# Dilated attention: near scores in the far scores' 64x32 tiles, scores and turns as one chain a block, values once per four blocks, bias as two loads a head

## The chip, the core and the metric

The kernel runs on one core of one Trainium2 chip. A core has a matrix engine (TensorE, "PE" in the profile; its weight loads are "PEld"), three engines for elementwise work (VectorE "DVE", ScalarE "ACT", GpSimd "POOL"), a queue that issues nearly all DMAs here (SyncE, "SP"), and 16 DMA engines that carry them. The metric is the device time of one execution in microseconds (us). Runs of one kernel are not equal: the three runs of the kernel before lie between 1393.0 and 1410.5 us.

## The reference

One block of a network on 1024 tokens of width 1024: a modulation from a condition vector, a norm, a projection into attention heads and gated delta-net heads, an output projection, and a gated feed-forward part. The change lies in the attention: 8 heads of 64, each with three dilated windows over the same keys, joined by a softmax over their log-sums. Cut to that:

```python
DILATED_BRANCHES = ((128, 1), (512, 4), (2048, 16))
...
def _dilated_branch(q, k, v, rel_bias, window, dilation):
    ...
    s = jnp.einsum('bhrnqd,bhrnkd->bhrnqk', qb * dh ** -0.5, kw) + bias[None, :, None, None]
    s = jnp.where(valid, s, NEG_INF)
    m = jnp.max(s, axis=-1, keepdims=True)
    e = jnp.exp(s - m)
    denom = jnp.sum(e, axis=-1, keepdims=True)
    o = jnp.einsum('bhrnqk,bhrnkd->bhrnqd', e, vw) / denom
    lse = (m + jnp.log(denom))[..., 0]
...
    w = jax.nn.softmax(jnp.stack(lses), axis=0)
    o = jnp.sum(w[..., None] * jnp.stack(outs), axis=0)
```

The three branches together are one softmax in which a key that lies in several windows counts several times. The kernel computes it so: score plus a bias that holds the relative bias and the logarithm of the count, one exponential, one sum, one product with the values.

## The kernel before

Everything is float32. Large products run as three matmuls of a split into high and low parts ("gemm", L575). The attention is worked in 4 pairs of heads, and in each pair in 8 blocks of 128 queries: 32 blocks. Heads 0 and 1 of a pair (`e` in the code) lie in partitions 0 to 63 and 64 to 127 of the tiles `q` and `k`. Within a block the 128 tokens are stored by class: token 4j + r stands at position 32r + j.

A block goes through three functions.

- `att_score` (L1317) makes the scores. A block's *near* keys are its own 128 and the 128 before: one matmul a head (L1330), a 64x128 tile of the array and 256 columns (128 in block 0). From block 2 on there are *far* keys, which only reach queries of their own class: four matmuls a head (L1336), each a 64x32 tile of one class r and 32n columns for block n. In the profile each such float32 matmul is two instructions. Then DVE adds the bias tile `bt` and takes a minimum (L1344, the scores are negated), ACT makes the exponential and the sum (L1348), DVE the reciprocal (L1349), POOL scales (L1350). The result is a tile `X` a head. Scores take their PSUM banks in turn from three.
- `att_turn` (L1358) transposes the pieces of `X` on PE (L1367, one to four a head and block) and copies them out of PSUM into a tile `et` (L1368; ACT for head 0 of the pair, DVE for head 1).
- `att_value` (L1373) multiplies with the values (L1399): parts of the near keys with `va`, parts of the far keys, class by class, with `vf`. It is called after every second block; the near parts of two blocks each time, the far parts of four blocks every second time. Four blocks share one PSUM bank, and after each four the bank is copied out (L1412 or L1416 and L1417).

`attend` (L1419) runs over 35 steps: the score of block i, the turn of block i - 1 (AT = 1), the values of block i - 3 (AV = 3). Before each step the function `ahead` puts a portion of gemm work into the program: projections that are left over, later the output projection (`out_delta`). A scheduler orders the instructions of each engine at compile time by the program's order and by what is ready. `tc.issue_after(x)` puts an instruction behind `x` on its engine; `urgent()` lets one go ahead of others. In `att_score` the matmuls of a block hang on each other in this way, in the order far classes, near head 0, near head 1; the matmuls of a value call as well; the turns do not.

The bias comes from a table. A matmul makes a row of 1152 values a head (L179), DVE negates it, three stores put it into HBM (`R_d`, L329). Eight copies within HBM write each head's row 32 times (`Rb_d`, L1124; from 70.7 us on in the profile). `att_bias` (L1273) then loads a head's tile `bt` from there with 15 DMAs (L1280), one of them for the far part (L1282), whose source address pattern leads with four repeats of the same rows. `att_load` (L1290) fetches q, k, the bias, `va` and `vf` for a pair; the next pair's load is called from the third block of a pair on. The values were stored by `va_evac` (L1088, stores at L1095), two stores a block of tokens and half.

Long before, between 68 and 111 us, the weights `wr_qd` and `wr_kd` of the delta-net's projections are loaded (L214), cast by ACT (L215) and completed by POOL (L216); between these casts ACT and POOL make the parts `hh` and `hl` of the normed input (L454, L461, L464).

Of the kernel before, what the change touches and what calls it, by code (L numbers as in the profile page):

```python
# [36 lines left out]
XB, ETB, AT, AV = 6, 4, 1, 3  # L37
# [31 lines left out]
def build(tc, I, out):  # L69
# [91 lines left out]
    tbl = start("tbl", "qd", [33, T]), start("tbl2", "qd", [33, P])  # L161
# [4 lines left out]
    for t, cs in zip(tbl, (slice(0, T), slice(T, T + P))):  # L166
        nc.sync.dma_start(t, I["tbl"][:, cs])
# [5 lines left out]
    R_d = dr.tile([8, 1152], F32, name="R_d")  # L173
    Rb_d = dr.tile([8, 32, 1152], F32, name="Rb_d")
    Rss = []
    for j in range(3):
        n = min(HALF, 1152 - HALF * j)
        ps = tbank(f"ps_R{j}")
        nc.tensor.matmul(  # L179
            ps[:8, 0:n], rb, tbl[j // 2][:, HALF * (j % 2) : HALF * (j % 2) + n], start=True, stop=True  # L180
        )
# [144 lines left out]
    for j, Rs in enumerate(Rss):  # L326
        n = min(HALF, 1152 - HALF * j)
        with tc.issue_after(loads[0].ins):
            nc.sync.dma_start(R_d[:, HALF * j : HALF * j + n], Rs[:, 0:n])  # L329
# [185 lines left out]
    class _:  # L515
        qk = scratch("qk", 8, [P, T])
        va = scratch("va", 2, [2, P, TB, P])
# [570 lines left out]
    def va_evac(c):  # L1088
        def f(tb, ps):
            t = pv.tile([P, 256], F32, name=f"va{c}_{tb}", tag="ev", bufs=4)  # L1090
            with urgent():
                taken[0] = nc.scalar.copy(t, ps[:, 0:256])
            with held():
                for i in range(2):
                    nc.sync.dma_start(  # L1095
                        bass.AP(
                            tensor=_.va[c].tensor, offset=_.va[c][i, 0:1, tb].offset,
                            ap=[[TB * P, 32], [32 * TB * P, 4], [1, P]],
                        ),
                        t[:, i * P : i * P + P],  # L1100
                    )
        return f
# [15 lines left out]
    def va_end(c):  # L1118
        f = va_evac(c)

        def g(tb, ps):
            f(tb, ps)
            if c == 0:
                nc.sync.dma_start(Rb_d[tb], R_d[tb : tb + 1, :].to_broadcast([32, 1152]))  # L1124
# [148 lines left out]
    def att_bias(h):  # L1273

        bt = pa.tile([P, HALF], F32, name=f"bt{h}", tag="bt", bufs=4)
        nc.gpsimd.memset(bt[:, 192:224], BIG)
        base, W = _.R[h, 0:1, :].offset, 1152

        def load(dst, at, ap):
            nc.sync.dma_start(dst, bass.AP(tensor=_.R.tensor, offset=base + at, ap=ap))  # L1280

        load(bt[:, 0:192], 3 * 288 + 31, [[0, 4], [W - 1, 32], [1, 192]])  # L1282
        for r in range(4):
            near = bt[32 * r : 32 * r + 32, 224:480].rearrange("p (d r j) -> p r d j", d=2, r=4)
            for a, b, at in ((0, r + 1, (3 - r) * 288 + 223), (r + 1, 4, 224)):
                for d in range(2 if a < b else 0):
                    load(near[:, a:b, d], at + 32 * d, [[W - 1, 32], [288, b - a], [1, 32]])
        return bt

    def att_load(hp):  # L1290
# [4 lines left out]
        bts = [att_bias(2 * hp + e) for e in range(2)]  # L1295
        va = pa.tile([P, TB, P], F32, name=f"va{hp}", tag="va", bufs=2)
        src = _.va[hp // 2][hp % 2]
        nc.sync.dma_start(va, src)
        vf = pa.tile([P, 2, 4, P], F32, name=f"vf{hp}", tag="vf", bufs=2)
        for c in range(2):  # L1300
            for n in range(4 - 2 * c):
                nc.sync.dma_start(
                    vf[32 * n : 32 * n + 32, c],
                    bass.AP(
                        tensor=src.tensor, offset=src[0:1, 4 * c + n].offset,
                        ap=[[TB * P, 32], [32 * TB * P, 4], [1, P]],
                    ),
                )
        return q, k, va, vf, bts
# [7 lines left out]
    def att_score(hp, n):  # L1317

        q, k, va, vf, bts = loaded[hp]
# [3 lines left out]
        rows = [slice(64 * e, 64 * e + 64) for e in range(2)]  # L1323
        parts = [(r, e) for r in (range(4) if f else ()) for e in range(2)] + [(None, 0), (None, 1)]
        mm = None
        with turn(f"S{hp}_{n}"):
            for r, e in parts:
                with tc.issue_after(mm.ins) if mm else ExitStack():
                    if r is None:
                        mm = nc.tensor.matmul(  # L1330
                            pss[e][:, f:w], q[rows[e], n * P : n * P + P], k[rows[e], b0 * P : n * P + P],
                            start=True, stop=True,
                        )
                    else:
                        qs = slice(32 * r, 32 * r + 32)
                        mm = nc.tensor.matmul(  # L1336
                            pss[e][qs, 0:f].rearrange("p (m j) -> p m j", j=32),
                            by_class(q[rows[e]])[:, n, r], by_class(k[rows[e]])[:, 0:n, r], start=True, stop=True,
                        )
        X = []  # L1340
        for e in range(2):
# [3 lines left out]
                out=x[:, 0:w], in0=pss[e][:, 0:w], in1=bts[e][:, 480 - w : 480], scale=1.0, scalar=3e38,  # L1345
# [8 lines left out]
        return X  # L1354
# [3 lines left out]
    def att_turn(hp, n, e, X):  # L1358
        h, f = 2 * hp + e, far(n)
        if n % 4 == 0:  # L1360
            turned[h] = pa.tile([P, 4, 4, P], F32, name=f"et{h}_{n // 4}", tag="et", bufs=ETB)
        s0, s1 = (1, 2) if n == 0 else (0, 2 + (n > 1) + (n > 5))
        cols = {0: f, 1: f + (P if n else 0), 2: 0, 3: P}
        ps = tbank(f"tr{h}_{n}")
        with turn(f"et{h}_{n}"):
            for i in range(s0, s1):
                nc.tensor.transpose(ps[:, i * P : i * P + P], X[:, cols[i] : cols[i] + P], ident)  # L1367
        (nc.vector.tensor_copy if e else nc.scalar.copy)(  # L1368
            turned[h][:, n % 4, s0:s1].rearrange("p b q -> p (b q)"), ps[:, s0 * P : s1 * P]
        )  # L1370
        return turned[h]

    def att_value(hp, n, ets):  # L1373

        q, k, va, vf, bts = loaded[hp]
        if n % 4 == 1:
            ybanks[hp] = ybank(f"y{hp}_{n}")
        yps = ybanks[hp]
# [3 lines left out]
        for m in (n - 1, n):  # L1382
            for i in range(0 if m else 1, 2):
                parts.append((slice(0, P), lambda e, b=m - 1 + i: va[:, b, 64 * e : 64 * e + 64],
                              m % 4, lambda e, m=m, i=i: ets[e][:, m % 4, i]))
        if n % 4 == 3:
            for c, n0, kr in ((0, 2 - 2 * half, 64 + 64 * half), (1, 2, 64))[: 1 + half]:
                for r in range(4):
                    qs = slice(32 * r, 32 * r + 32)
                    parts.append((slice(0, kr), lambda e, c=c, r=r: vf[:, c, r, 64 * e : 64 * e + 64],  # L1390
                                  (slice(n0, 4), qs), lambda e, n0=n0, c=c, qs=qs: ets[e][:, n0:4, 2 + c, qs]))
        mm = None
        with turn(f"y{hp}_{n}"), urgent():
            for i, (ks, w, at, mov) in enumerate(parts):
                for e in (1, 0):
                    es_ = slice(64 * e, 64 * e + 64)
# [664 lines left out]
```

## Time and profile before

| | |
|---|---|
| median of 3 runs | 1402.5 us (1393.0 to 1410.5) |
| the profiled execution | 1403.9 us, span 1402.0 us |
| PE busy | 1354.4 us, 97% of the span |
| DVE, ACT, POOL busy | 839.6, 619.5, 241.4 us |
| mean granted clock of TensorE | 0.978 |
| first and last attention score on PE (L1330) | 487.0 and 697.8 us |

The engines' busy times are shares of one span, so an engine at 97% is the bound, with the reservation that matmuls overlap and their ends are modelled. In a timeline row the first number is the start in us from the beginning of the span, the second the length; `x16` says that 16 like instructions in a row are merged, and a bracket at the end names the idle time before it and what ended it. In a table of windows each row has the stretch, its length, the busy time of PE, PEld, DVE, ACT and POOL with the number of instructions, the granted clock, the busy share of the DMA engines and GB/s; a window asked for one line of code alone shows only that line's engines. A row of waits names the instruction that waited, what ended the wait, the sum in us, how many times, and the longest.

### The profile page before, as it was taken

How to read it: one execution, taken by the hardware profiler on the slowest of the kernel's cores; microseconds unless marked ns; L12 is line 12 of the kernel's file. 1: busy time of each engine (PE TensorE's matmuls, PEld its weight loads, DVE VectorE, ACT ScalarE, POOL GpSimd, SP SyncE). 2: the span in 40 equal slices, each digit the busy share in tenths (PEclk: the TensorE clock that was granted, in tenths of full speed). 3: DMA queues.
4: the chain of work that ended last, by engine and by line, in shares of the span. 5: the costliest groups of instructions: out<-in, count | busy, mean ns of one | idle time of the engine just before them, and what ended most of it. 6: DMA issues, size and time to landing. Idle time of an engine off the chain costs nothing.

```text
span 1402.0 us, 24478 instructions
## 1 busy us (share of the span) xinstructions
PE 1354.4 (97%) x9056; PEld 1093.6 (78%) x9056; DVE 839.6 (60%) x1604; ACT 619.5 (44%) x1237; POOL 241.4 (17%) x252
## 2 busy tenths in 40 slices
PE   8998999999999999999999999999999999999998
PEld 4777787888888867666677878888888888888876
DVE  3688573555833422254428987667585776474497
ACT  4497424246222233344457743333333333444455
POOL 2345303324211322223353000000000000000000
PEclk9999999999966999999999999999999999999999
DMA  8636674365432244464474355545463665776685
GB/s 308 223 95 174 171 223 132 128 209 154 132 103 80 82 114 133 121 196 133 135 253 138 121 164 168 172 150 173 135 203 107 209 215 181 259 224 196 195 262 195
DMA packets 181422, 237.12 MB, mean 169 GB/s; under 512 B 42838, under 2 KB 88199, under 8 KB 181304
## 3 DMA queue, kind: packets, MB, share of 16 engines
q1 hardware_dynamic: 181304, 235.57, 53.6%
q8 instruction: 71, 1.16, 0.4%
q14 instruction: 47, 0.39, 0.1%
HBM read 172.75 MB, written 63.94 MB: 169 GB/s over the span
## 4 chain that ended last, share of the span: by engine, by line
PE 55%; DVE 4%; DMA 2%; issue 1%; ACT 1%; SPq 1%; POOL 0%; POOLq 0%; DVEq 0%; ACTq 0%
PE wua L1655 9%; PE wga L1655 8%; PE X L1855 6%; PE wgc L1655 4%; PE wuc L1655 4%; PE wo L575 4%; PE g_a L575 4%; PE Z L1855 3%; PE y L1399 2%; PE wgb L1655 2%; PE Y L1855 2%; PE wub L1655 2%; PE S L1330 2%; PE tr L1367 2%; SPq L1280 1%
## 5 line engine op out<-in xcount | busy, mean ns | idle before, releaser
L1645 DVE TENSOR_TENSOR wl_db<-wr_db,wh_db 128x512 fp32r<-128x512 f32 x77 | 52.8, 689 | 66.5 <-ACT wh_db L1644 66.5
L1344 DVE CUSTOM_DVE_ANT_0 X<-S,bt 128x128 f32<-128x128 f32 (+7 forms) x64 | 31.7, 517 | 99.6 <-PE S L1330 64.9
L1644 ACT CAST wh_db<-wr_db 128x512 fp32r<-128x512 f32 x77 | 47.5, 621 | 87.2 <-PE X L1855 36.3
L1855 PE MATMUL X<-wl_db,wh_da 128*128 128x512 f32 x160 | 62.4, 390 | 0.3 <-DVE wl_db L1645 0.3
L1855 PE MATMUL X<-wh_db,wl_da 128*128 128x512 f32 x160 | 62.3, 389 | 0.0
L1855 PE MATMUL X<-wh_db,wh_da 128*128 128x512 f32 x160 | 62.2, 389 | 0.0
L1348 ACT ACTIVATE X<-X,sc 128x128 f32<-128x128 f32 (+7 forms) x64 | 37.1, 581 | 47.8 <-DVE sc L1344 47.7
L1645 DVE TENSOR_TENSOR wl_da<-wr_da,wh_da 128x512 fp32r<-128x512 f32 x77 | 52.7, 685 | 2.7 <-ACT wh_da L1644 2.7
L1644 ACT CAST wh_da<-wr_da 128x512 fp32r<-128x512 f32 x77 | 47.5, 616 | 13.4 <-DMA wr_da<-ao_d 7.4
L575 PE MATMUL wo<-yh,wh_wo 128*128 128x512 f32 x128 | 52.9, 413 | 0.0
L575 PE MATMUL g_a<-hh,wh_a 128*128 128x512 f32 x128 | 51.7, 404 | 0.1
L575 PE MATMUL wo<-yl,wh_wo 128*128 128x512 f32 x128 | 51.2, 400 | 0.0
L575 PE MATMUL g_a<-hl,wh_a 128*128 128x512 f32 x128 | 51.0, 399 | 0.0
L575 PE MATMUL wo<-yh,wl_wo 128*128 128x512 f32 x128 | 50.9, 398 | 0.0
L575 PE MATMUL g_a<-hh,wl_a 128*128 128x512 f32 x128 | 50.1, 391 | 0.0
L1350 POOL TENSOR_SCALAR X<-X,sc 128x128 f32<-128x128 f32 (+7 forms) x64 | 35.8, 564 | 81.2 <-DVE sc L1349 69.0
L1644 ACT CAST wh_wg_s<-wg_s 128x512 fp32r<-128x512 f32 x33 | 20.6, 623 | 56.1 <-PE wuc L1655 23.8
L216 POOL TENSOR_TENSOR wl_wo<-wr_wo,wh_wo 128x512 fp32r<-128x512 f32 x24 | 31.6, 1316 | 59.3 <-ACT wh_wo L215 59.3
L601 PE MATMUL g_z<-wh_z,hh 128*128 128x256 f32 x128 | 37.2, 291 | 3.7 <-ACT zt L622 3.7
L601 PE MATMUL g_va<-wh_va,hh 128*128 128x256 f32 x128 | 40.2, 314 | 0.0
L601 PE MATMUL g_va<-wl_va,hh 128*128 128x256 f32 x128 | 40.1, 313 | 0.0
L1644 ACT CAST wh_wu_s<-wu_s 128x512 fp32r<-128x512 f32 x33 | 20.4, 622 | 43.7 <-PE wga L1655 17.2
(550 smaller groups left out, 4208.1 us busy)
## 6 DMA issues: line engine op xcount, KB each, us to landing
wm<-in_wada SPq DMA_DIRECT2D x44, 512.0 KB
wr_da<-ao_d SPq DMA_DIRECT2D x77, 256.0 KB
wr_wu<-in_wu SPq DMA_DIRECT2D x50, 256.0 KB
wr_wg<-in_wg SPq DMA_DIRECT2D x48, 256.0 KB
ao_d<-a SPq DMA_DIRECT2D x44, 256.0 KB
wr_wd<-in_wdn SPq DMA_DIRECT2D x44, 256.0 KB
wr_db<-wt_d SPq DMA_DIRECT2D x44, 256.0 KB
ao_d<-as SPq DMA_DIRECT2D x33, 256.0 KB
```

The lines of the kernel that those rows point to most:

```text
L216: (eng or nc.gpsimd).tensor_tensor(out=lo[:, :n], in0=raw[:, :n], in1=hi[:, :n].bitcast(F32), op=ALU.subtract)
L575: last[0] = nc.tensor.matmul(ps, a[:, w0], b[k0 + k4][:, cs], start=(i == 0), stop=(i == n - 1))
L601: last[0] = nc.tensor.matmul(ps[:, :n], a[k][:, ts_], b[:, w0], start=(i == 0), stop=(i == 23))
L1330: mm = nc.tensor.matmul(pss[e][:, f:w], q[rows[e], n * P : n * P + P], k[rows[e], b0 * P : n * P + P], start=True, stop=True,)
L1344: nc.vector.tensor_tensor_reduce(out=x[:, 0:w], in0=pss[e][:, 0:w], in1=bts[e][:, 480 - w : 480], scale=1.0, scalar=3e38, op0=ALU.add, op1 ...
L1348: nc.scalar.activation(x[:, 0:w], x[:, 0:w], AF.Exp, scale=-1.0, bias=sc[:, 0:1], accum_out=sc[:, 2:3])
L1350: nc.gpsimd.tensor_scalar(out=x[:, 0:w], in0=x[:, 0:w], scalar1=sc[:, 3:4], scalar2=0.0, op0=ALU.mult, op1=ALU.add)
L1367: nc.tensor.transpose(ps[:, i * P : i * P + P], X[:, cols[i] : cols[i] + P], ident)
L1644: nc.scalar.copy(hi, src)
L1645: (eng or nc.vector).tensor_tensor(out=lo, in0=src, in1=hi.bitcast(F32), op=ALU.subtract)
L1655: nc.tensor.matmul(ps, a[:, w0], b, start=(first and k == 0 and n_ == 0), stop=(k == 3 and n_ == 2), skip_group_check=True,)
L1855: nc.tensor.matmul(bank[b], a[:, ts_], w, start=(first and n_ == 0), stop=(last and n_ == 2), skip_group_check=True,)
```

## The change

- The near scores are made like the far ones: four 64x32 tiles a head, one a class, 256 columns each. All score matmuls of a block hang on each other, head 1 before head 0.
- The transposes of a block hang on each other too, and on the last score matmul of the step, so that a step has one chain: scores of block i, then turns of block i - 2 (AT = 2, with 8 `X` buffers in place of 6).
- Values are made once per four blocks, and for far keys always with all 128 rows; rows that hold no key are zero in two fixed buffers `vf0` and `vf1`.
- The bias table is laid out in 4 rows of 736 values, one a class, and copied in HBM so that a head's tile can be read with one step between partitions: two loads a head. The copies are wider (768 values a row, 129 rows a head). The tile `bt` holds both heads of a pair and lies in another pool (`pr`, the slots `xp`).
- The value store is one DMA in place of two; the next pair's load is called one block later.

```diff
-XB, ETB, AT, AV = 6, 4, 1, 3
+XB, ETB, AT, AV = 8, 4, 2, 3
...
-    R_d = dr.tile([8, 1152], F32, name="R_d")
-    Rb_d = dr.tile([8, 32, 1152], F32, name="Rb_d")
+    R_d = dr.tile([8, 4, 736], F32, name="R_d")
+    Rb_d = dr.tile([8, P + 1, 768], F32, name="Rb_d")
...
-    for j, Rs in enumerate(Rss):
-        n = min(HALF, 1152 - HALF * j)
-        with tc.issue_after(loads[0].ins):
-            nc.sync.dma_start(R_d[:, HALF * j : HALF * j + n], Rs[:, 0:n])
+    with tc.issue_after(loads[0].ins):
+        for r in range(4):
+            for j in range(2):
+                nc.sync.dma_start(
+                    R_d[:, r, 224 + 256 * j : 480 + 256 * j], Rss[j][:, 64 * (3 - r) : 64 * (3 - r) + 256]
+                )
+            nc.sync.dma_start(R_d[:, r, 0:224], Rss[2][:, 0:224])
...
-                for i in range(2):
-                    nc.sync.dma_start(
...
+                nc.sync.dma_start(
+                    bass.AP(
+                        tensor=_.va[c].tensor, offset=_.va[c][0:1, tb].offset,
+                        ap=[[TB * 256, 32], [32 * TB * 256, 4], [1, 256]],
+                    ),
+                    t,
+                )
...
-                nc.sync.dma_start(Rb_d[tb], R_d[tb : tb + 1, :].to_broadcast([32, 1152]))
+                nc.sync.dma_start(
+                    bass.AP(
+                        tensor=Rb_d.tensor, offset=Rb_d[tb, 0:1, :].offset + 96,
+                        ap=[[32 * 768 - 32, 4], [768, 32], [1, 736]],
+                    ),
+                    bass.AP(tensor=R_d.tensor, offset=R_d[tb, 0:1, :].offset, ap=[[736, 4], [0, 32], [1, 736]]),
+                )
...
-    def att_bias(h):
...
+    def att_bias(hp):
+
+        bt = pr.tile([P, 2, HALF], F32, name=f"bt{hp}", tag="xp", bufs=2)
+        nc.gpsimd.memset(bt[:, :, 192:224], BIG)
+        for e in range(2):
+            at = _.R[2 * hp + e, 0:1, :].offset + 127
+            for dst, ap in ((bt[:, e, 0:192], [[767, P], [1, 192]]), (bt[:, e, 224:480], [[767, P], [64, 8], [1, 32]])):
+                nc.sync.dma_start(dst, bass.AP(tensor=_.R.tensor, offset=at + (0 if len(ap) == 2 else 224), ap=ap))
         return bt
+
+    vfs = []
+    for i in range(2):
+        vfs.append(pa.tile([P, 3, 4, P], F32, name=f"vf{i}", tag=f"vf{i}"))
+        nc.gpsimd.memset(vfs[i][64:128, 1:3], 0.0)
...
-                if qb >= 2 and hp < 3 and hp + 1 in done and hp + 1 not in loaded:
+                if qb >= 3 and hp < 3 and hp + 1 in done and hp + 1 not in loaded:
```

The scores, the turns and the values:

```diff
-            for r, e in parts:
-                with tc.issue_after(mm.ins) if mm else ExitStack():
-                    if r is None:
-                        mm = nc.tensor.matmul(
-                            pss[e][:, f:w], q[rows[e], n * P : n * P + P], k[rows[e], b0 * P : n * P + P],
-                            start=True, stop=True,
-                        )
...
+            for near in range(0 if f else 1, 2):
+                for r in range(4):
+                    for e in (1, 0):
+                        rows, qs = slice(64 * e, 64 * e + 64), slice(32 * r, 32 * r + 32)
+                        if near:
+                            out, src = pss[e][qs, f:w], k[rows, b0 * P : n * P + P]
+                        else:
+                            out = pss[e][qs, 0:f].rearrange("p (m j) -> p m j", j=32)
+                            src = by_class(k[rows])[:, 0:n, r]
+                        with tc.issue_after(mm.ins) if mm else ExitStack():
+                            mm = nc.tensor.matmul(out, by_class(q[rows])[:, n, r], src, start=True, stop=True)
...
+        pss = [tbank(f"tr{2 * hp + e}_{n}") for e in range(2)]
+        with turn(f"et{hp}_{n}"):
+            for e in (1, 0):
+                for i in range(s0, s1):
+                    with tc.issue_after(mm.ins) if mm else ExitStack():
+                        mm = nc.tensor.transpose(
+                            pss[e][:, i * P : i * P + P], X[e][:, cols[i] : cols[i] + P], ident
+                        )
...
-        for m in (n - 1, n):
+        for m in range(n, n - 4, -1):
             for i in range(0 if m else 1, 2):
...
-        if n % 4 == 3:
-            for c, n0, kr in ((0, 2 - 2 * half, 64 + 64 * half), (1, 2, 64))[: 1 + half]:
...
+        for c, n0, slot in ((0, 0, 2), (1, 2, 3)) if half else ((2, 2, 2),):
+            for r in range(4):
+                qs = slice(32 * r, 32 * r + 32)
+                parts.append((lambda e, c=c, r=r: vf[:, c, r, 64 * e : 64 * e + 64], (slice(n0, 4), qs),
+                              lambda e, n0=n0, slot=slot, qs=qs: ets[e][:, n0:4, slot, qs]))
...
-                ets[i - AT] = [att_turn(hp, qb, e, xs[i - AT][e]) for e in range(2)]
+                ets[i - AT] = att_turn(hp, qb, xs.pop(i - AT)[0], xs[i][1] if i in xs else None)
...
-            if i >= AV and units[i - AV][1] % 2:
+            if i >= AV and units[i - AV][1] % 4 == 3:
```

More of the change, by code (lines that the diff above doesn't have):

```diff
@@ L1419, in attend @@
+        hi = natural(yh[hp][:, cs])
+        nc.scalar.copy(hi, src)
+        nc.vector.tensor_tensor(out=natural(yl[hp][:, cs]), in0=src, in1=hi.bitcast(F32), op=ALU.subtract)
     def attend(switch):
@@ L1986, in _bucket_table @@
 def _bucket_table():
[L1988 removed]
+    i = np.arange(64)
+    near = [128 * (1 - q) + 4 * (31 - i) + 3 - t for q in range(2) for t in range(7)]
+    d = np.concatenate([*near, 4 * (255 - np.arange(224))])
     dist_f = np.maximum(d, 1).astype(np.float32)
```

137 lines of the change are left out of this document (47 added, 90 removed).

## The prediction

> **What bounds the kernel now.** I read the engine table of the page first, then the table of windows for the attention stage, the waits of that stage, and the timeline of TensorE inside it.
>
> ```profile
> PE 1354.4 (97%) x9056; PEld 1093.6 (78%) x9056; DVE 839.6 (60%) x1604; ACT 619.5 (44%) x1237; POOL 241.4 (17%) x252
> 485.50:705.04 219.54, 215.64 (x1619) 148.15 (x1617) 76.07 (x255) 84.98 (x225) 65.62 (x91) 1.00 0.49 138
> 485.50:705.04 219.54, 126.21 (x488) 87.47 (x488) 1.00 0.49 138
> 667.00 0.39 PE L575 MATMUL wo<-yl,wh_wo 128*128 128x512 f32 x1
> 669.27 0.39 PE L575 MATMUL wo<-yh,wl_wo 128*128 128x512 f32 x1
> ```
>
> TensorE is the bound, and in the attention stage (485.50 to 705.04) it is busy for 215.6 of 219.5 us while DVE, ACT and POOL stay below 85. But a busy PE includes draining. The second window row holds the gemm matmuls (L575) alone: 488 of them. Undisturbed, ten follow each other in 669.27 - 667.00 = 2.27 us, 0.227 us each, so all the gemm work of the stage is worth 488 x 0.227 = 110.8 us. The other 219.5 - 110.8 = 108.7 us is what 32 attention blocks cost, 3.4 us a block. That is the figure the change works on.
>
> ```profile
> PEld S L1330 <- issue: 9.4, 36, 0.4
> PEld tr L1367 <- issue: 7.7, 26, 0.4
> PEld S L1336 <- issue: 7.0, 27, 0.4
> PEld y L1399 <- DVE et L1368: 5.4, 11, 0.7
> PEld y L1399 <- issue: 4.1, 17, 0.4
> PEld y L1399 <- DVE sc L1349: 3.3, 10, 0.4
> PEld tr L1367 <- POOL X L1350: 2.8, 7, 0.6
> PEld S L1336 <- DVE sc L1344: 2.6, 3, 2.1
> PEld g_a L575 <- issue: 2.5, 13, 0.3
> PEld wo L575 <- issue: 1.7, 9, 0.3
> 677.82 0.40 PE L1336 MATMUL S<-raw,raw 64*32 64x96 f32 x16
> 678.14 0.70 PE L1330 MATMUL S<-raw,raw 64*128 64x256 f32 x4
> 678.78 0.87 PE L1367 MATMUL tr<-ident,X 128*128 128x128 f32 x6
> 679.41 0.48 PE L575 MATMUL wo<-yh,wh_wo 128*128 128x512 f32 x1
> 679.72 0.40 PE L575 MATMUL wo<-yl,wh_wo 128*128 128x512 f32 x1
> 512.63 0.70 PE L1330 MATMUL S<-raw,raw 64*128 64x256 f32 x2
> 513.25 0.70 PE L1399 MATMUL y<-et,va 128*64 128x128 f32 x8
> 513.88 0.70 PE L1330 MATMUL S<-raw,raw 64*128 64x256 f32 x2
> 514.51 0.87 PE L1367 MATMUL tr<-ident,X 128*128 128x128 f32 x6
> ```
>
> Weight loading stands still for 9.4 + 7.7 + 7.0 + 4.1 + 2.5 + 1.7 = 32.4 us, 128 times 0.25 us, for nothing that the profile shows ("issue"), each time where the tile shape in the column after the operands changes (64\*32, 64\*128, 128\*128, 128\*64). Another 5.4 + 3.3 + 2.8 + 2.6 = 14.1 us waits for results. The rows from 677.82 are a block in order; those from 512.63 one torn apart: the score of one head (x2), then values, then the score of the other head. Half the near score, 2 instructions, holds PE from 512.63 to 513.25, 0.62 us, as long as the whole one (678.14 to 678.78, 0.64), since two heads run beside each other in the array and a half runs alone.
>
> **The change, part by part.** *Near scores in 64x32 tiles.* The cost of a far score grows with its columns:
>
> ```profile
> 569.05 0.70 PE L1330 MATMUL S<-raw,raw 64*128 64x256 f32 x4
> 568.78 0.34 PE L1336 MATMUL S<-raw,raw 64*32 64x64 f32 x16
> 545.02 0.61 PE L1336 MATMUL S<-raw,raw 64*32 64x224 f32 x16
> 545.56 0.70 PE L1330 MATMUL S<-raw,raw 64*128 64x256 f32 x4
> 675.19 0.66 PE L1399 MATMUL y<-et,va 128*64 128x128 f32 x8
> 675.78 0.50 PE L575 MATMUL wo<-yl,wh_wo 128*128 128x512 f32 x1
> 516.93 0.68 PE L1399 MATMUL y<-et,vf 64*64 64x64 f32 x16
> 517.54 0.50 PE L575 MATMUL g_a<-hl,wh_a 128*128 128x512 f32 x1
> ```
>
> 64 columns take 569.05 - 568.78 = 0.27 us, 224 take 0.54: 1.67 ns a column plus 0.16 for the switch that follows. No row shows 256 near columns in such tiles. Either they run at that slope (0.43 us), or the array stays as now (0.64 with its switch); the 224-column row is the nearest, I take the slope. Per pair of heads, blocks 0 to 7: now near 7 x 0.64 + 0.41, far 0.27 + 0.32 + 0.38 + 0.44 + 0.49 + 0.54 (the slope between the two rows), and 8 entries from a gemm at 0.09 (the 0.31 us from 679.41 to 679.72 against 0.227 shows such a surcharge), 8.0 us. After: 0.16 + 1.67 ns x (far + near columns), 0.37, 0.59, 0.69, 0.75, 0.80, 0.85, 0.91, 0.96, and 0.7 for entries, 6.6 us.
>
> *Turns.* 46 transposes a pair at 0.63 / 6 = 0.105 (678.78 to 679.41), 4.9 us, before and after.
>
> *Values once per four blocks.* Eight matmuls (two parts) hold PE for 0.59 us, so a part is 0.21 and the switch 0.16; a 64-column part is half (0.61 for four with the switch). Now, four calls a pair: 3 parts; 4 and 4 short; 4; 4 and 4 far and 4 short: 5.9 us with six switches, and 4 entries at 0.1. After, two calls: 7 and 4 short, 8 and 4 and 4 short, one shape throughout: 5.2, and 2 entries. The zero rows of the far values cost nothing, the columns set the time.
>
> So a pair, untorn, costs 8.0 + 4.9 + 6.3 = 19.2 us now and 6.6 + 4.9 + 5.4 = 16.9 after; four pairs 76.7 and 67.7. Counting alone gives 9 us. The other 108.7 - 76.7 = 32 us are torn blocks, extra switches and waits. The chain (score, then the turn of two blocks earlier, in fixed order) should remove much: two switches a block and two a value call make 80 in place of 128, 48 x 0.25 = 12 us; and a turn whose X is two blocks old no longer waits. Values still wait for the copies behind the last turn, and a late gemm can still get in between. I take 17 of the 32. The ends are a gain of 9 (nothing removed) and 41 (all): **26 us**.
>
> [...]
>
> *What the chain makes wait.* The chained turn stands behind the score on PE, the score behind its bank, and the bank behind the other block's L1344 on DVE. The first score of the chain takes the bank that comes free last, and the turns of the block before (0.6 to 0.85 us) and 2 us of gemm a block cover the DVE step. DVE at 76 of 219 us is far from a bound. Values come in two larger bursts; ACT and DVE read their bank as often as now.
>
> *Bias and loads on SP.* Bias issues fall from 120 to 16, value stores from 32 to 16; the first table's stores rise from 3 to 12, the vf loads from 24 to 32: 103 fewer.
>
> ```profile
> L1280 SPq DMA_DIRECT2D bt<-Rb_d x120: 315/427/1470, 483.8 to 640.0; - x120
> 497.14 0.29 DVE L1344 CUSTOM_DVE_ANT_0 X<-S,bt 128x128 f32<-128x128 f32 x1 [17.66 <-DMA bt<-Rb_d]
> 506.40 0.68 PE L1336 MATMUL S<-raw,raw 64*32 64x64 f32 x16 [1.69 <-DVE sc L1344]
> ```
>
> At 0.43 us that is 44 us of SP. DVE waits 17.7 us for the first bias, but PE runs gemms meanwhile and idles 1.69 us in all: I take 1 us, and keep 0 to 3. Moving the next pair's loads one block later and the fixed vf buffers leave six blocks of lead; behind a vf load that waits on SP stand weight loads, with three raw buffers to cover them.
>
> *The wider table.* This is the part that costs. Each head's copy within HBM (L1124) grows from 144 KB to 4 x 32 x 736 x 4 = 377 kB, and its address pattern now leads with 4 instead of 32.
>
> ```profile
> 77.10:81.70 4.60, 4.60 (x22) 3.77 (x22) 2.70 (x8) 4.52 (x8) 0.00 (x0) 1.00 0.76 221
> 485.85:486.80 0.95, 0.95 (x6) 0.64 (x4) 0.00 (x0) 0.23 (x1) 0.95 (x2) 1.00 0.31 92
> 75.38 4.28 SPq L1124 DMA_DIRECT2D Rb_d<-R_d  x7
> 96.78 0.61 ACT L215 CAST wh_kd<-wr_kd 128x512 fp32r<-128x512 f32 x1
> 101.24 0.50 PE L575 MATMUL g_qd<-hl,wh_qd 128*128 128x512 f32 x1 [0.71 <-POOL hl L464]
> ```
>
> Seven copies now run at 221 GB/s with 0.76 of the 16 DMA engines busy. The second row is the far bias load, whose source already leads with 4: 0.31 of the engines, 92 GB/s. At that rate a copy takes 4.1 us and the seven, issued from 75.4 on, end at 104, where the kd slab lands about 1.5 us later. Its cast stands on ACT at 96.78, ahead of the splits of hh and xt that PE waits for at 101.24. ACT would stand for some 9 us and PE for 8. At 221 GB/s the copies end at 87 and cost nothing; at four engines of the rate above (221 / 0.76 / 16 x 4 = 73) they end at 112, a stall of 16. The window of the far load is the nearest row: **+8 us**, ends 0 and 16.
>
> [...]
>
> Sum on the profiled execution (1403.9 us, span 1402.0): 1403.9 - 26 - 1 + 8 = 1384.9. It stands 1.4 above the median of the runs, 1402.5, so **1384 us**.
>
> **The rivals.** *All the waste goes* (-41): 1403.9 - 41 - 1 + 8 - 1.4 = 1368. For it: TensorE waits for little else. Against: values wait for copies and sums of DVE, L1399 21 times in the rows above, and are still behind the turns. *The copy is hidden*: 1375. For it: order on ACT is fixed at compile time and may put the kd cast later. Against: the cast stands where it is because the slab is ready. *The chain does not bind* (it fixes an order but lets gemms in between, only the 9 us remain): 1403.9 - 9 - 1 + 8 - 1.4 = 1400. For it: value matmuls are chained already and are torn all the same. *Slower*: the copies' writes, at a longer stride, run at half the far load's rate: 8.2 us each, end at 133, a stall of 37, 1412. It decides from 27 us of stall, 6.9 us a copy (55 GB/s). Against: no row shows four engines below 73.
>
> **How the numbers follow.** Forecast 42%, all waste gone 15%, copy hidden 17%, chain without effect 20%, slower 6%. The forecast's own range is 1376 to 1393. 1366 to 1403 takes in the rivals at 1368, 1375 and 1400 and leaves out the slow one and the tails. About 2% (1374) is what a measurement of this kernel can tell from no change. Faster by more: all waste gone (13 of 15), half the hidden-copy cases (8), a tail of the forecast (5): 0.26. Slower by over 2% needs 56 us of stall: 0.02. Within 2%: 0.72.
>
> **What would show it.** Between the first score and the last value: 488 gemms and about 190 us in place of 219.5; "issue" waits near 80; scores in runs of 32 in one shape, at most 0.96 us to the turn. In the table's copies: the DMA share near 0.25 from 71 to 104 us and a wait of ACT for the kd slab. The prediction is wrong if scores still show in halves, if the near part takes more than 0.45 us, or if ACT does not stand still before 105 us.

## The result, and the profile after

| | before | after |
|---|---|---|
| median of 4 runs each | 1397.7 us (1388.8 to 1410.5) | 1459.0 us (1454.4 to 1464.5) |
| ratio to before, 95% interval | | 1.046 (1.038 to 1.054) |
| profiled execution: span | 1402.0 us | 1455.7 us |
| last `g_va` matmul of the delta-net phase | 485.4 us | 561.9 us |
| last value matmul of the attention | 704.8 us | 757.6 us |

The change makes the kernel slower by 4.6%. The prediction said 1384 us, range 1366 to 1403. Here and below, ratios are formed from fast runs alone: a run more than 1.5% above the fastest of its kernel, as the one of 1410.5 us is here, is left out of them.

The page of the kernel after: busy time, the slices of PE and the granted clock.

```profile
PE 1339.3 (92%) x9440; PEld 1091.4 (75%) x9440; DVE 841.9 (58%) x1604; ACT 623.1 (43%) x1240; POOL 239.5 (16%) x250
PE   8998765989847999999999999999999999999998
PEclk9998787979978999999999999999999999999999
```

PE is still the busiest engine, but at 92% of the span in place of 97%. A slice is 36.4 us: the idle ones and those with a low clock lie among slices 4 to 13, some 110 to 470 us. That is not the attention, which begins at 563 us, but the delta-net phase ahead of it. The table of windows divides the two. First the kernel before, delta-net phase only:

```profile
90.00:485.40 395.40, 371.82 (x3470) 325.04 (x3469) 233.26 (x490) 167.77 (x368) 122.00 (x108) 0.92 0.48 142
```

Then the kernel after, the delta-net phase, the attention stage, and the gemm matmuls of that stage alone:

```profile
90.00:561.90 471.90, 379.17 (x3462) 328.09 (x3461) 232.82 (x488) 171.12 (x369) 119.40 (x107) 0.87 0.43 127
561.90:757.60 195.70, 192.62 (x2009) 141.38 (x2007) 76.01 (x255) 84.07 (x227) 67.43 (x91) 1.00 0.49 150
561.90:757.60 195.70, 126.33 (x493) 89.02 (x493) 1.00 0.49 150
```

The attention stage fell from 219.5 to 195.7 us. With its gemms taken out at 0.227 us each it fell from 108.7 to 195.7 - 493 x 0.227 = 83.8 us, by 24.9. The prediction had counted 26 for the change itself and 1 for the loads of the bias. The delta-net phase does the same work in both kernels (3470 and 3462 recorded matmuls), and grew from 395.4 to 471.9 us. PE stood idle for 23.6 us of it before and for 92.7 after; the other 7 us are busy time, at a clock of 0.87 in place of 0.92. What follows the attention is the same (697.2 and 698.1 us). So +76.5 - 23.7 + 0.9 makes the 53.7 us between the spans (by the times in the table above, the attention took 219.4 us before).

The longest waits of PE in this phase, after:

```profile
PE trv L861 <- ACT vd L543: 20.8, 4, 9.8
PE g_z L602 <- ACT sp_qd L1111: 15.4, 1, 15.4
PE kk_q L785 <- DMA qd<-cv_d: 14.3, 1, 14.3
PE g_kd L576 <- ACT wh_kd L213: 7.0, 1, 7.0
```

Before, the longest sum in that phase is 3.9 us. Three of the four name ACT as what PE waited for, one a load. Part of the reason shows in SP's waits. Before, from 90 to 460 us:

```profile
SPq L214 <- POOL wl_qd L216: 30.8, 7, 13.6
SPq L1137 <- PE mods L196: 28.6, 11, 17.3
...
SPq L214 <- POOL wl_va L216: 18.8, 7, 5.8
...
SPq L214 <- POOL wl_a L216: 6.5, 4, 2.5
```

(Between these rows stand waits of SP for results of the delta net, 21.5 us for `R` the longest.) After, the same stretch:

```profile
SPq L1143 <- PE mods L194: 86.9, 12, 23.9
SPq L212 <- POOL wl_va L214: 32.0, 3, 30.4
SPq L212 <- POOL wl_qd L214: 20.9, 4, 14.8
SPq L212 <- POOL wl_a L214: 20.5, 1, 20.5
```

These are loads of weights for later work (`wm` for the modulation, `wr_va`, `wr_a`) that stand at the head of SP's queue and wait until a buffer is free. What stood behind them on SP was held up too, in one case for 20.6 us. The timeline of the kernel after shows it:

```profile
384.37 3.48 SPq L212 DMA_DIRECT2D wr_a<-in_wd  x3
406.46 5.09 ACT L756 ACTIVATE dt<-dt,lr 128x128 f32<-128x128 f32 x17
411.43 0.62 ACT L213 CAST wh_a<-wr_a 128x512 fp32r<-128x512 f32 x1
412.13 1.26 POOL L214 TENSOR_TENSOR wl_a<-wr_a,wh_a 128x512 fp32r<-128x512 f32 x1 [3.57 <-ACT wh_a L213]
413.42 0.33 SPq L212 DMA_DIRECT2D wr_a<-in_wd  x1
414.32 0.42 SPq L1231 DMA_DIRECT2D cv_d<-cv  x1
414.83 0.44 SPq L1250 DMA_DIRECT2D qd<-cv_d  x1
420.20 3.78 PE L785 MATMUL kk_q<-qd,kd 64*128 64x128 f32 x32 [14.28 <-DMA qd<-cv_d]
```

Read it from the end. PE is idle for 14.3 us until the load of `qd` lands. That load is issued at 414.8, behind the fourth load of `wr_a` at 413.4. This one waits for a buffer that POOL frees when it has made `wl_a`; POOL waits for a cast on ACT at 411.4, and the cast stands on ACT behind a row of 17 `dt` steps. SP did nothing from 392.8 to 413.4. `wr_a` is a weight that the attention's projection wants later; `qd` is what PE wants now, and ACT had finished the `cv` that it is loaded from at 397.2.

Not every wait hangs on a prefetch. The 15.4 us of `g_z` end on ACT: its step `cv` waits 13.1 us for a store (`tn_d<-tt`), and the copy `sp_qd` that PE needs stands behind it. The rows that lead to `trv` were not followed to their start.

### The profile page after: what moved, and what is told of

It reads as the page before. It is cut to its first block, busy times and chain, and to the rows that moved or that the text cites. A ratio compares the mean times of both kernels' runs of the same rounds, so it can differ in the third digit from the quotient of the medians.

```text
span 1455.7 us, 25071 instructions
## 1 busy us (share of the span) xinstructions
PE 1339.3 (92%) x9440; PEld 1091.4 (75%) x9440; DVE 841.9 (58%) x1604; ACT 623.1 (43%) x1240; POOL 239.5 (16%) x250
## 5 line engine op out<-in xcount | busy, mean ns | idle before, releaser
L602 PE MATMUL g_z<-wh_z,hh 128*128 128x256 f32 x128 | 40.7, 318 | 21.6 <-ACT sp_qd L1111 15.4
L1643 ACT CAST wh_wg_s<-wg_s 128x512 fp32r<-128x512 f32 x33 | 20.5, 622 | 58.2 <-PE wuc L1654 24.9
L602 PEld LDWEIGHTS g_z<-wh_z,hh 128*128 128x128 f32 x128 | 28.2, 220 | 23.0 <-ACT sp_qd L1111 15.6
L602 PE MATMUL g_z<-wh_z,hl 128*128 128x256 f32 x128 | 39.9, 312 | 0.0
L602 PE MATMUL g_z<-wl_z,hh 128*128 128x256 f32 x128 | 39.4, 308 | 0.0
```

Of the source, the lines that this page charges most:

```text
L602: last[0] = nc.tensor.matmul(ps[:, :n], a[k][:, ts_], b[:, w0], start=(i == 0), stop=(i == 23))
L1643: nc.scalar.copy(hi, src)
```

## The experiments

The change has one piece that lies ahead of all this in time: the wider bias table and its eight copies within HBM (L1124), whose address pattern leads with 4 instead of 32. In the profile before, all eight copies were issued between 70.7 and 79.1 us. In the profile after, they lie between 75.9 and 432.0 us. The experiments ran on three chips, with the kernel before beside them: its median was 1388.3 us beside e1 to e4, 1390.3 beside e5 to e8, and 1389.2 beside e9 and e10. The leading theory (A) was that the pattern makes the compile-time scheduler put all queues into another order, and that this order loses the time. The rivals: the bytes and stores of the wider table (B), transfers on few DMA engines that hold up others (B'), the attention's buffers and chains (C).

### The pattern, and the table, one at a time

**e1**, the changed kernel with the copies' pattern turned round:

```diff
-                        ap=[[32 * 768 - 32, 4], [768, 32], [1, 736]],
+                        ap=[[768, 32], [32 * 768 - 32, 4], [1, 736]],
...
-                    bass.AP(tensor=R_d.tensor, offset=R_d[tb, 0:1, :].offset, ap=[[736, 4], [0, 32], [1, 736]]),
+                    bass.AP(tensor=R_d.tensor, offset=R_d[tb, 0:1, :].offset, ap=[[0, 32], [736, 4], [1, 736]]),
```

> The changed kernel with one thing different: the address pattern of the eight copies of the bias table leads with 32 in place of 4; the same bytes (377 kB a copy) reach the same places. Between the first projection and the last gemm of the delta-net phase the changed kernel lost 76 us and won 24 in the attention. Theory A (the pattern that leads with 4 makes the compile-time scheduler put copies, loads and casts into another order, and that order loses the 76 us): the copies stand together again near 70 to 85 us, the last g_va matmul comes back from 562 to about 486-495 us, and the time is 1370 to 1385 us. Theory B (the wider table's bytes or its twelve stores cost the time, whatever the pattern): last g_va stays past 540, 1440 to 1460 us. Theory C (the rest of the change, bt in the slots xp, more X buffers, fixed vf, holds the delta-net phase up): 1450 to 1465 us.

Measured: **1353.3 us** (1352.0 to 1354.3), ratio to before 0.977 (0.973 to 0.981). Last `g_va` at 461.2 us. The whole loss is gone, and the time lies below the range that theory A gave. B and C fall. Theory A had two details wrong: the copies don't stand together by 85 us but lie between 77.2 and 146.5, and the last `g_va` came 25 us earlier than the earliest it gave. So this order isn't that of the kernel before either.

**e2**, the kernel before with its own copies led by 4, no byte more:

```diff
-                nc.sync.dma_start(Rb_d[tb], R_d[tb : tb + 1, :].to_broadcast([32, 1152]))
+                nc.sync.dma_start(
+                    bass.AP(
+                        tensor=Rb_d.tensor, offset=Rb_d[tb, 0:1, :].offset, ap=[[288, 4], [1152, 32], [1, 288]]
+                    ),
+                    bass.AP(tensor=R_d.tensor, offset=R_d[tb : tb + 1, :].offset, ap=[[288, 4], [0, 32], [1, 288]]),
+                )
```

> The kernel before with one thing different: the address pattern of its eight copies (147 kB each) leads with 4 in place of 32, in the pieces 4 x 32 x 288; the same bytes reach the same places. Theory A (the leading 4 alone changes the order of the queues): clearly slower than before although no byte is added, the last g_va matmul 20 to 80 us later than 485, 1420 to 1475 us; the copies stand spread over hundreds of us on SP. Theory B (bytes): the same as before within 1%, 1390 to 1410. Theory A' (the spread of copies is harmless, only the first loads' delay counts): 1395 to 1415.

Measured: 1436.1 us, ratio 1.035 (1.027 to 1.044); the copies lie between 69.9 and 344.5 us, last `g_va` at 515.1. A leading 4 alone makes the old kernel slower by 48 us (against 1388.3), at the old number of bytes.

**e3**, the kernel before with the new table, copies and bias loads, its scores, turns and values kept; **e4**, the changed kernel with the old table, copies and 15 bias loads a head. Their diffs are the parts of the change that concern `tbl`, `R_d`, `Rb_d` and `att_bias`, one way and the other; of e3:

```diff
-    R_d = dr.tile([8, 1152], F32, name="R_d")
-    Rb_d = dr.tile([8, 32, 1152], F32, name="Rb_d")
+    R_d = dr.tile([8, 4, 736], F32, name="R_d")
+    Rb_d = dr.tile([8, P + 1, 768], F32, name="Rb_d")
...
-        bts = [att_bias(2 * hp + e) for e in range(2)]
+        bt = att_bias(hp)
+        bts = [bt[:, e] for e in range(2)]
```

and of e4, against the changed kernel:

```diff
-    R_d = dr.tile([8, 4, 736], F32, name="R_d")
-    Rb_d = dr.tile([8, P + 1, 768], F32, name="Rb_d")
+    R_d = dr.tile([8, 1152], F32, name="R_d")
+    Rb_d = dr.tile([8, 32, 1152], F32, name="Rb_d")
```

> The kernel before with the change's bias table alone (twelve stores, wide copies that lead with 4, two bias loads a head, bt in the slots xp); scores, turns, values and va stores as before. Theory A and theory B alike: the whole loss without the gain, before + 70 to 80, 1465 to 1480 us; attention stage about 219 us. Theory C (loss from the attention's buffers and chains): 1395 to 1410 us.

> The changed kernel with the bias table of before (three stores, copies of 147 kB that lead with 32, fifteen bias loads a head, into the same slots xp); scores, turns, values as changed. Theory A and theory B: the gain without the loss, last g_va near 486, attention stage near 196 us, 1370 to 1385 us. Theory C: near 1455 us.

Measured: e3 1495.6 us, ratio 1.081 (1.071 to 1.090), above the range that was given, with the last `g_va` at 572.4, 10.5 us later than in the change, which stays unexplained; e4 1362.1 us, ratio 0.984 (0.978 to 0.990), last `g_va` at 461.6, both below what was given. The loss goes with the table, and most of the gain with the scores, turns and values. The new table itself isn't to blame: e1 has it and beats e4.

### What a copy takes on the chip

The same eight copies in three profiles, by the table of windows. A window is the time in which the packets of one copy run. The kernel after, then e1, then e2:

```profile
77.35:82.25 4.90, 4.90 (x23) 4.08 (x22) 2.98 (x9) 4.86 (x9) 0.00 (x0) 1.00 0.25 77
```

```profile
99.55:101.10 1.55, 1.55 (x8) 1.18 (x7) 0.65 (x1) 1.55 (x4) 1.55 (x2) 1.00 0.89 285
```

```profile
71.40:73.55 2.15, 2.15 (x26) 1.50 (x17) 2.15 (x4) 1.42 (x3) 1.33 (x2) 1.00 0.25 76
```

In these windows a copy of 377 kB led by 4 keeps a quarter (0.25) of the 16 engines busy for 4.9 us; led by 32, nearly all (0.89) for 1.6 us. Eight copies of 4.9 us are 39 us, at that share of the engines, spread over 360 us. If each stopped PE for its whole length, that would still be half of the 76 us lost. In e2 it would be 8 x 2.2 = 17 us for 48 lost (30 between the profiles' last `g_va`). Theory B' is weak by this, but it isn't out.

### The order by itself

**e9** and **e10** part the transfer from the order. The program is built twice. The first time, with one pattern of the copies, gives the order of the instructions on each engine and queue. The second time, with the other pattern, each instruction is tied behind its forerunner in that order, as `tc.issue_after` does (an order of issue, not a wait for the end):

```diff
-    with tile.TileContext(nc, schedule_with_timeline_sim=False) as tc:
-        build(tc, aps, out)
+        with tile.TileContext(nc, schedule_with_timeline_sim=False) as tc:
+            build(tc, aps, out)
+            traced = {i.name: i for i in nc.cur_bb.bb.instructions}
+            for names in (order or {}).values():
+                for x, y in zip(names, names[1:]):
+                    tc.add_manual_dep(
+                        traced[y], x,
+                        mybir.DependencyInfo(mybir.DependencyClass.NoSync, mybir.DependencyReason.DATA), reason="order",
+                    )
...
+    _, _, order = once(32)
+    nc, arrays, got = once(4, order)
```

That is e9; in e10 the 32 and the 4 change places.

> The changed kernel with its copies exactly as changed (they lead with 4), but every engine's and queue's instructions in the order that the compile-time scheduler gives when the copies lead with 32. Theory A (the order alone loses the time): as the kernel with copies that lead with 32, last g_va 455 to 470 us, 1350 to 1362 us. Theory B' (copies on four engines hold up what runs beside them, in whatever order): 1410 to 1460 us, or in between by the share that is the transfer's.

> The mirror of it: the copies lead with 32, and every engine's and queue's instructions stand in the order that the scheduler gives when they lead with 4 (the changed kernel's own order). Theory A: nothing comes back, last g_va 550 to 570 us, 1445 to 1465 us. Theory B': the time comes back, 1350 to 1385 us.

Measured: **e9 1357.8 us**, ratio 0.974 (0.966 to 0.983), last `g_va` at 462.4; **e10 1458.0 us**, ratio 1.046 (1.039 to 1.054), last `g_va` at 564.7. With copies led by 4 the good order is as fast as e1; with copies led by 32 the bad order is as slow as the change. The delta-net phase of e9 and e10 in the table of windows, e9 first:

```profile
90.00:461.00 371.00, 347.51 (x3459) 303.35 (x3458) 232.74 (x490) 166.59 (x366) 120.38 (x106) 0.99 0.55 160
```

```profile
90.00:562.00 472.00, 380.71 (x3447) 329.58 (x3446) 231.57 (x490) 170.61 (x367) 119.35 (x106) 0.87 0.43 126
```

Idle PE is 23.5 us in the one and 91.3 in the other. So the order accounts for the loss, and B' is out: at a given order the two patterns differ by 4.5 us (e9 against e1) and by 1.0 (the change against e10), in runs whose ranges overlap. These pairs ran on different chips, but their ratios to the kernel before agree too: 0.974 and 0.977, 1.046 and 1.046.

### Is it one kind of load?

**e5** asked whether the `wm` loads, SP's longest wait, are the cause: in the changed kernel they lose their mark "urgent" and so stand behind the small loads of the delta net.

```diff
-                with urgent(), tc.issue_after(last[0].ins if i + k0 > 0 else loads[0].ins), held():
+                with tc.issue_after(last[0].ins if i + k0 > 0 else loads[0].ins), held():
```

> The changed kernel (copies that lead with 4, 377 kB) with one thing different: the loads of the modulation's weights (wm, L1143) are no longer marked urgent, so that the compile-time order puts them behind the small loads of the delta net (dt, lt) on SP. In the changed kernel SP stands 86.9 us behind wm loads whose buffer PE has not yet freed (21.5 us with copies that lead with 32). Theory A1 (the new order of the SP queue loses the time, and wm loads at its head are the larger part of it): the copies still take some 5 us each, but SP's wait for mods falls below 45 us, the last g_va comes 30 to 70 us earlier than 562, 1385 to 1430 us. Theory A2 (the order of other instructions, the weight slabs wr and their casts, loses it): SP waits as long, for other releasers, 1440 to 1470 us. Theory B' (the copies' four engines hold up other loads on the chip): 1440 to 1470 us as well, whatever SP waits for.

Measured: 1445.8 us, ratio 1.037 (1.029 to 1.046), last `g_va` at 551.1. SP's waits of e5, from 90 to 550 us:

```profile
SPq L212 <- POOL wl_va L214: 38.8, 5, 30.4
SPq L212 <- POOL wl_z L214: 35.4, 7, 15.8
SPq L1044 <- DVE o L1054: 34.9, 11, 12.0
SPq L892 <- DVE tt L889: 32.3, 1, 32.3
...
SPq L1143 <- PE mods L194: 13.8, 4, 10.0
```

From 90 to 550 us the wait behind `wm` fell from 101.5 us in the change to 13.8, and only 13 us of time came back: other loads now stand at the head of the queue. Theory A1 (chiefly `wm`) falls; A2 had the time right, and so had B', which e9 rules out. So it is not this one kind of load; e9 and e10 changed the order as a whole, and which parts of it cost how much was not divided further. In e1 the same loads as in the case above lie like this in the timeline of SP:

```profile
311.00 0.33 SPq L1231 DMA_DIRECT2D cv_d<-cv  x1
...
315.49 0.32 SPq L1231 DMA_DIRECT2D cv_d<-cv  x1
316.63 0.32 SPq L1250 DMA_DIRECT2D qd<-cv_d  x1
319.93 0.33 SPq L212 DMA_DIRECT2D wr_a<-in_wd  x1
320.36 0.38 SPq L1250 DMA_DIRECT2D qd<-cv_d  x1
```

`cv_d` and the first load of `qd` go ahead of the `wr_a` load here, and nothing stands for longer than 3 us.

### The parts of the attention's gain

On top of e1 one part each was put back; the last `g_va` then lies between 458.5 and 464.9 us, against 461.2 in e1. **e6**, near scores as one 64x128 tile a head:

```diff
-                for r in range(4):
+                for r in range(1 if near else 4):
...
+                        lhs = by_class(q[rows])[:, n, r]
                         if near:
-                            out, src = pss[e][qs, f:w], k[rows, b0 * P : n * P + P]
+                            out, src = pss[e][:, f:w], k[rows, b0 * P : n * P + P]
+                            lhs = q[rows, n * P : n * P + P]
```

> The kernel with copies that lead with 32 (1353 us, attention stage from the last g_va to the last value 195.5 us), and the near scores again as one 64x128 tile a head behind the far ones, in the same chain. Delta-net phase in the same order. Theory T1 (as the prediction counted: the near part is cheaper in 64x32 tiles, and a switch of shape a block goes): stage longer by 5 (count alone) to 14 us (with a switch in each of 24 blocks with far keys), 1358 to 1367 us. Theory T2 (the shape of the near part is worth nothing, the gain is in the order of turns and values): stage within 3 us, 1350 to 1356.

**e7**, turns one block after their score and hung on nothing:

```diff
-XB, ETB, AT, AV = 8, 4, 2, 3
+XB, ETB, AT, AV = 8, 4, 1, 3
...
-                    with tc.issue_after(mm.ins) if mm else ExitStack():
-                        mm = nc.tensor.transpose(
-                            pss[e][:, i * P : i * P + P], X[e][:, cols[i] : cols[i] + P], ident
-                        )
+                    nc.tensor.transpose(pss[e][:, i * P : i * P + P], X[e][:, cols[i] : cols[i] + P], ident)
```

> The kernel with copies that lead with 32, and the turns again one block after their score (AT = 1) and hung on nothing; near scores in 64x32 tiles, values per four blocks as changed. Theory T1 (torn blocks and turns that wait for their X are what the chain removed): stage longer by 8 to 17 us, more switches (issue waits above 90 in place of 77), 1361 to 1370 us. Theory T2 (the chain does not bind): within 3 us.

**e8**, near values after every second block:

```diff
-        for m in range(n, n - 4, -1):
+        for m in (n, n - 1):
...
-            if i >= AV and units[i - AV][1] % 4 == 3:
+            if i >= AV and units[i - AV][1] % 2:
```

> The kernel with copies that lead with 32, and the near values again after every second block (far values after every fourth, with the fixed buffers as changed). Theory T1 (as counted, 0.9 us a pair, and eight fewer bursts to wait for): stage longer by 3 to 8 us, 1356 to 1361 us. Theory T2 (values once per four blocks are worth nothing by themselves): within 2 us.

Measured as the length of the attention stage, gemms out at 0.227 us:

| | time, us | stage, us | gemms in it | rest, us | against e1 |
|---|---|---|---|---|---|
| e1 | 1353.3 | 195.5 | 493 | 83.6 | |
| e6, near as 64x128 | 1358.9 | 198.3 | 491 | 86.8 | +3.2 |
| e7, turns free | 1356.6 | 199.6 | 494 | 87.5 | +3.9 |
| e8, values per two blocks | 1357.8 | 199.7 | 488 | 88.9 | +5.3 |
| e4, old table and bias loads | 1362.1 | 202.0 | 493 | 90.1 | +6.5 |

In e6 the waits of weight loading say where it goes:

```profile
PEld S L1341 <- issue: 16.5, 52, 0.4
PEld tr L1372 <- issue: 8.9, 27, 0.3
```

52 standstills at scores in place of 33 in e1: 19 more, where 24 blocks have far keys and so one switch of shape more. All its "issue" standstills sum to 29.5 us, e1's to 26.4, which is the whole difference of 3.2; the count had 4 x 1.4 = 5.6 us for this part. e6's time lies in the range of its first theory, its stage (2.8 us longer) in that of its second. In e7 the stage grew by 4.1 us, half of the least that its first theory asked and more than its second allowed, and its standstills did not rise (25 and 29 at turns and scores); what is longer in it are waits for results (3.2 us of turns for their `X`, 1.3 in e1), which fits the lead of two blocks better than the fixed chain; the two were not parted. e8 fits its first theory. The four differences add up to 18.9 of the 25.1 us that e1 gained (108.7 - 83.6). The other 6 belong to no part alone. Each row is one profiled execution: the unaltered attention gives 83.6 to 85.0 us in e1, the change, e9 and e10, so a difference of some 3 us stands above that spread, but its size is rough.

## Why the prediction was wrong

**The attention: right in sum.** 26 us were predicted, and 1 for the loads of the bias; 23.8 were measured for both (24.9 by the gemm count). The stage was put near 190 us with 488 gemms and took 195.7 with 493. That the sum came out is in part luck, since the loads of the bias gave more than their 1 us (below), and so the scores, turns and values less than their 26: some 18 to 22. The waits of weight loading in it, after:

```profile
PEld S L1339 <- issue: 11.7, 34, 0.4
PEld tr L1370 <- issue: 11.2, 28, 0.4
PEld y L1400 <- issue: 1.5, 4, 0.4
...
PEld wo L576 <- issue: 1.4, 6, 0.4
...
PEld g_a L576 <- issue: 1.4, 5, 0.4
```

These are 77 standstills where 80 were forecast. But one is 0.35 us now and was 0.25, so they sum to 27.2 us in place of 32.4, a gain of 5 where 12 had been taken. The near scores fit:

```profile
738.14 0.93 PE L1339 MATMUL S<-raw,raw 64*32 64x160 f32 x32
739.01 0.87 PE L1370 MATMUL tr<-ident,X 128*128 128x128 f32 x6
...
746.97 1.04 PE L1339 MATMUL S<-raw,raw 64*32 64x224 f32 x32
747.99 0.52 PE L1370 MATMUL tr<-ident,X 128*128 128x128 f32 x3
```

32 instructions in one shape, 0.87 us to the turn in block 5 and 1.02 in block 7, where 0.85 and 0.96 were worked out from the slope of the far scores; in the first and third pair of heads every block lies within 0.02 us of its figure. The 1.02 is past the 0.96 that the prediction allowed (its near part takes 1.02 - 0.16 - 224 x 1.67 ns = 0.49, past 0.45), and three of the 32 blocks still show their scores in parts (from 655.9, 665.4 and 739.8 us): two signs against itself that the prediction had named. So the lengths of the scores were well counted; the split between counted work and waste was not tested well by the sum.

**Bias loads on SP: too small.** 1 us was taken, 0 to 3 kept. Between e4 and e1, which differ by the table and its loads, the stage with its gemms taken out differs by 6.5 us. Between the kernel before and e3, the same step with the old attention, it differs by 3.0 (216.3 us with 487 gemms in e3).

**The wider table: this step failed.** The prediction said that "this is the part that costs" and priced it as transfers: seven copies at the far load's rate, 4.1 us each, that delay the load of the kd slab, ACT standing for 9 us, +8. The transfer itself was nearly right, with 4.9 us a copy at 0.25 of the engines. The four engines at 73 GB/s, from which the upper end of 16 us was worked out, were the author's estimate, and no row of the profile before shows them; the windows above show 0.25 of the 16 engines at 77 GB/s for a copy led by 4, and 0.89 at 285 GB/s for one led by 32. What failed is the frame around it: the step kept SP's order of before ("issued from 75.4 on") and let only the durations change. In the profile after, one copy was issued there; the second came at 108.5 us, and the third at 197.1. From 90 to 105 us PE was busy for 15.0 of 15.0 us, and ACT never waited for the slab, which the prediction had named as a sign against itself. The cast that the step named did hold PE up, but later and for another reason:

```profile
91.48 5.22 SPq L212 DMA_DIRECT2D wr_kd<-in_wd  x3
113.88 1.65 ACT L213 CAST wh_kd<-wr_kd 128x512 fp32r<-128x512 f32 x3
114.55 0.80 PE L576 MATMUL g_kd<-hh,wh_kd 128*128 128x512 f32 x1 [7.03 <-ACT wh_kd L213]
```

The first three of the slab's four loads were issued from 91.5 us, not later than before (93.3). The cast stood at 113.9 on ACT in place of 96.8, behind work on `kd`, `qd` and `kt` that was put ahead of it, and PE waited 7.0 us. That this is near the forecast's 8 is chance: the slab was not late, and it is 7 of the 92.7 us that PE stood idle. In place of +8 the phase grew by 76.5 us. With equal transfers the two orders differ by 1458.0 - 1353.3 = 105 us (e10 against e1) and by 1459.0 - 1357.8 = 101 (the change against e9).

**The rivals.** One of them ("the copy is hidden") said that the order on ACT is fixed at compile time and may change, but only as a chance to hide the copy, for one cast, and as a gain. The cast did come later, and it was a loss. The slower rival looked for a slow transfer and gave it 6%; no term asked what a different order of all queues would be worth.

**The base.** Without the failed step the forecast was 1376. e1, which is that case, took 1353. Part of the rest is the profile that the sum was made against: its delta-net phase holds 371.8 us of PE work at a mean clock of 0.92, which e1 does in 346.8 at 0.99:

```profile
90.00:461.20 371.20, 346.84 (x3467) 302.69 (x3466) 229.96 (x489) 167.39 (x368) 120.11 (x107) 0.99 0.55 159
```

That is 25 us that one execution spent on the same work at a lower clock. The row also shows what the bad order costs in full: against e1 the phase of the changed kernel has 92.7 - 24.4 = 68 us more of idle PE and 379.2 - 346.8 = 32 us more of busy PE, the same work at a clock of 0.87 in place of 0.99. In these profiles more idle time goes with a lower clock (92.7 and 91.3 us of it at 0.87, 24.4 and 23.5 at 0.99), but idle time alone does not decide: the kernel before has 23.6 at 0.92. The runs of the kernel before that stand beside e1 differ by their clock too: they lie between 1379.9 us, at a mean clock of 0.996 over the whole execution, and 1408.3, at 0.971. The one at 0.996, which is e1's clock as well, is 26.6 us above e1; the forecast without the failed step had 27. That is a single run, and where in the others the clock was low, no profile here shows.

The cause is open one step further back. That the scheduler puts the copies elsewhere because it reckons a longer time for a pattern that leads with 4 is inferred from its orders (e1 against the change, e2 against before); its reckoning itself was not looked at.

## What to carry to other kernels

Where a scheduler fixes the order of the queues at compile time, the address pattern of a DMA can be an input to that order, and a small edit far from the bound can move the loads behind it (here the two orders lay 105 us apart, e10 against e1): compare the order of SP's queue, and of the casts and copies on ACT, before and after a change, before you reckon with durations. Price a changed DMA twice, once as bytes on the chip and once as its place among the loads of its queue, and give the second its own rival. When a phase whose work was not touched grows, look for prefetches at the head of the DMA queue that wait for a buffer, and hold the order fixed to test it.

## What the hardware showed besides

In the profile of the kernel before, the granted clock stayed low through work that the profile shows as unbroken. PE waited 1.3 us for a load, until 395.6 us, and then:

```profile
400.00:440.00 40.00, 40.00 (x482) 33.55 (x472) 10.17 (x22) 8.54 (x22) 3.16 (x4) 0.50 0.29 86
```

40 us of 40 busy by the profile, all of them at a clock of 0.50. The whole stretch at 0.50 lasts 47.8 us, from 397.1 to 444.9, and holds small tiles (32x32, 64x64 and 128x32) among larger ones. In e1 the same instructions ran at 1.00, 221 ns a `lw` matmul against 315. What decides between the two, these runs do not show.
